# Norms between layers: tokens times the scale vector, turned by products with a diagonal of the tokens' factors

## The chip, the cores and the metric

The kernel runs on one core of a Trainium2 chip. The metric is the time of one execution in device microseconds (us). The engines are TensorE (PE in the profile, with its weight loads as PEld), VectorE (DVE), ScalarE (ACT), GpSimd (POOL) and SyncE (SP, which issues most DMAs). SBUF is the memory on the core, PSUM the one that TensorE writes its products to.

## The reference

One launch computes two transformer blocks on 256 tokens of 1024 features. The first has two layers (a mixture of block attention and compressed attention, then a forgetting attention) with a squared-ReLU MLP each; the second a gated MLP, a hybrid of differential attention and a state-space scan, and another gated MLP. All of it is in 32-bit floats. What matters here is the norm that stands between one layer and the next:

```python
def rmsnorm(x, g):
    xf = x.astype(jnp.float32)
    y = xf * lax.rsqrt(jnp.mean(xf * xf, axis=-1, keepdims=True) + RMS_EPS)
    return (y * g.astype(jnp.float32)).astype(x.dtype)

    for layer in range(DEPTH):
        hn = rmsnorm(h, mix_norm[layer])
        ...
        h = h + moba_nsa_mixer(hn, ...)
        ...
        h = h + sqrelu_mlp(rmsnorm(h, mlp_norm[layer]), mlp_w1[layer], mlp_w2[layer])
```

Each token is divided by the root of its mean square (one factor per token), multiplied by a vector of 1024 gains (one per feature), and goes into the next layer's first product. In the second block the branch is normed too before it is added to h.

## The kernel before

The residual x lies in SBUF with the tokens on the partitions, as two halves t = 0 and t = 1 of 128 tokens. A product on TensorE sums over partitions, so a layer's input has to be turned: features on the partitions, tokens along the row. The turned input `xx` has eight chunks of 128 features, each twice: a rounded part and a rest (`split`, L386 to 388: ACT copies the rounded part, DVE subtracts it for the rest), because all large products run in a reduced 32-bit type (fp32r) as a sum of rounded-by-rounded, rounded-by-rest and rest-by-rounded. Weights stream in by chunks of 1 MB (`raw`, DMA from SP), and are split likewise into `whi` (ACT, L387) and `wlo` (DVE, L388). Each product is issued by `mm` (L214). Fp32r products of 512 columns and of 256 columns make up nearly all of PE's work.

Between two layers:

- `finish` (L967) ends a layer: the last products of t = 0 (`part(0)`), its `epi`, the last products of t = 1, the turn of t = 0, the `epi` of t = 1. It leaves the turn of t = 1 as `late_turn` to the next layer.
- `epi` adds the layer's products to x (L990, or scales by a further norm, L427, in the second block), and calls `prenorm` (L431). It takes the sum of squares of the two 512-feature halves on ACT (`xn<-x`, L410), adds the two and the epsilon on DVE (`ms`, L423), raises that to -1/2 on POOL (`rs<-ms`, L416), and multiplies x by that factor and the gain on DVE, each half in one instruction (`xn<-x,rs,gain`, L427).
- `turn` (L391) turns xn chunk by chunk: PE transposes four chunks of 128x128 into one PSUM bank (L397, `ps_p<-cst,xn` or `ps_b<-cst,xn`, where cst holds the identity), then `split` writes them to xx; twice for eight chunks.
- `begin` (L310 on) starts the next layer: it runs the first three weight groups on t = 0, two of them into the bank pair ps_o and the third into a ps_b bank, then calls `late_turn`, then runs the three on t = 1.

There are six such boundaries (two token halves each, twelve turns). The first norm of the program, the state-space part's own norm and the output's are made elsewhere.

The tile framework's scheduler sets the order of instructions on each engine ahead of the run, from dependencies, its own cost estimates and priorities: `soon(300)` raises the priority of the turns and epis. Each engine then works its list strictly in that order. Buffers come from pools with a fixed count: P tiles (128x384) nine (`PB`), xn two, ps_b four banks, ps_p two.

Of the kernel before, what the change touches and what calls it, by code (L numbers as in the profile page):

```python
# [12 lines left out]
OP = mybir.AluOpType  # L13
# [7 lines left out]
PB = 9  # L21
# [93 lines left out]
class Kern:  # L115
# [274 lines left out]
    def turn(self, src, xx, k0, t, n=4, tag="b", than=None):  # L390


        w = min(n, 4)
        for b in range(0, n, w):
            ps = self.bank(tag)
            for k in range(w):
                i = self.nc.tensor.transpose(ps[:, k * 128:k * 128 + 128],  # L397
                                             src[:, (b + k) * 128:(b + k) * 128 + 128], self.ident)
                if than is not None:
                    self.later(i, than)  # L400
            s = slice(k0 + b, k0 + b + w)
            self.split(xx[:, s, t * 128:t * 128 + 128], xx[:, s, 256 + t * 128:256 + t * 128 + 128],
                       ps[:, :w * 128].rearrange("p (k n) -> p k n", k=w))
# [25 lines left out]
    H = (slice(0, 512), slice(512, 1024))  # L429

    def prenorm(self, t, G, eps):  # L431
        x = self.x[:, t, :]
        xn = self.t([128, 1024], "xn", 2)
        r = self.rstd([x[:, s] for s in self.H], xn, eps)
        for s in self.H:
            self.scaled(xn[:, s], x[:, s], r, G[:, s])
        return xn

    def first_norm(self, t, G, eps):

# [1229 lines left out]
```

## Time and profile before

| | us |
|---|---|
| median of 3 runs | 1206.33 (1205.54 to 1206.60) |
| the profiled execution | 1205.98 |
| its span, first to last instruction | 1203.6 |
| mean granted clock of TensorE | 0.999 of full |

The page gives for each engine the time in which it was busy; a line of the timeline has the start, the time taken by the group, the engine, the line of the kernel, the operation, output and inputs by their names, the shapes and the count of instructions, and in brackets how long the engine had been idle before and what ended that. PE is the engine with the most busy time; the end of a matrix product is modelled, so that two products in a row overlap in the trace. The rows that matter stand two sections below.

### The profile page before, as it was taken

The numbers are of one execution on the slowest core, as the hardware profiler recorded it, in microseconds if no ns is written. First come the engines' busy times: TensorE is split into PE (matmuls) and PEld (weight loads), VectorE is DVE, ScalarE is ACT, GpSimd is POOL, SyncE is SP. The second block draws the span as 40 slices with busy tenths as digits, with TensorE's granted clock in tenths as the row PEclk, the third lists the DMA queues.
The fourth block names the chain that finished last, engine by engine and source line by source line (L and its number), as shares of the span: only waits on it lengthen the run. The fifth ranks groups of instructions, "written<-read, shape, count | busy, mean of one in ns | idle before, by whom it ended". The sixth has DMA issues, their size and how long they took to land.

```text
span 1203.6 us, 17736 instructions
## 1 busy us (share of the span) xinstructions
PE 1176.9 (98%) x6890; PEld 1002.3 (83%) x6890; DVE 795.7 (66%) x1442; ACT 658.5 (55%) x1221; POOL 86.8 (7%) x119
## 2 busy tenths in 40 slices
PE   8999999999999999999999999999999999999997
PEld 6878688888887878888888888887987778888886
DVE  6685666666667657566657665676888876666663
ACT  5675554545455645454546555564764755555552
POOL 2200000000000000000002000003234020000000
PEclk9999999999999999999999999999999999999999
DMA  8645255555456334555544655562543235555550
GB/s 300 227 159 192 106 192 177 194 189 187 165 197 241 106 118 176 183 205 177 197 186 154 237 178 202 180 222 95 199 151 123 88 135 181 187 197 180 199 182 35
DMA packets 32245, 210.71 MB, mean 175 GB/s; under 512 B 3761, under 2 KB 4561, under 8 KB 8226
## 3 DMA queue, kind: packets, MB, share of 16 engines
q1 hardware_dynamic: 29360, 201.06, 47.1%
q0 software_dynamic: 2512, 8.27, 2.1%
q8 instruction: 54, 0.88, 0.3%
q10 hardware_dynamic: 290, 0.27, 0.1%
q14 instruction: 29, 0.24, 0.1%
HBM read 208.22 MB, written 1.09 MB: 174 GB/s over the span
## 4 chain that ended last, share of the span: by engine, by line
PE 85%; DVE 6%; ACT 3%; issue 2%; POOL 1%; DMA 1%; SPq 0%; POOLq 0%; DVEq 0%; ACTq 0%
PE ps_b L214 39%; PE ps_p L214 26%; PE ps_o L214 15%; DVE wlo L388 2%; PE ps_o L218 2%; ACT whi L387 1%; PE ps_b L538 1%; PE ps_p L397 1%; DMA raw<-in_w_e 1%; ACT xn L410 1%; ACT P L561 1%; DVE xn L427 1%; POOL rs L416 1%; DMA T<-c_dram 1%; PE ps_b L397 0%
## 5 line engine op out<-in xcount | busy, mean ns | idle before, releaser
L388 DVE TENSOR_TENSOR wlo<-raw,whi 128x1024 fp32r<-128x1024 f32 (+1 forms) x365 | 443.5, 1233 | 232.8 <-ACT whi L387 232.0
L387 ACT ACTIVATE whi<-raw 128x1024 fp32r<-128x1024 f32 (+1 forms) x367 | 376.7, 1048 | 182.2 <-PE ps_p L214 89.6
L214 PE MATMUL ps_b<-xx,whi 128*128 128x512 f32 x1024 | 361.5, 394 | 0.0
L214 PE MATMUL ps_b<-xx,wlo 128*128 128x256 f32 x1024 | 289.1, 282 | 0.0
L214 PEld LDWEIGHTS ps_b<-xx,whi 128*128 128x128 f32 x1024 | 192.3, 188 | 43.8
L214 PEld LDWEIGHTS ps_b<-xx,wlo 128*128 128x128 f32 x1024 | 192.5, 188 | 1.7
L214 PE MATMUL ps_p<-xx,whi 128*128 128x256 f32 (+2 forms) x800 | 146.1, 286 | 0.6 <-DVE fz L1284 0.5
L214 PEld LDWEIGHTS ps_p<-xx,whi 128*128 128x128 f32 (+2 forms) x800 | 120.9, 185 | 5.9 <-issue 4.1
L214 PE MATMUL ps_p<-xx,wlo 128*128 128x256 f32 x384 | 108.2, 282 | 0.0
L214 PE MATMUL ps_b<-whi,xx 128*128 128x256 f32 (+2 forms) x440 | 102.5, 320 | 1.4 <-ACT xx L387 1.4
L214 PE MATMUL ps_p<-whi,xx 128*128 128x512 f32 x232 | 82.9, 414 | 1.6 <-DVE xx L388 1.0
L416 POOL TENSOR_TENSOR rs<-ms,mhalf 128x1 f32<-128x1 f32 x22 | 14.8, 672 | 903.8 <-DVE ms L423 894.6
L214 PEld LDWEIGHTS ps_b<-whi,xx 128*128 128x128 f32 x440 | 73.2, 188 | 7.7 <-ACT xx L387 1.6
L214 PEld LDWEIGHTS ps_p<-xx,wlo 128*128 128x128 f32 x384 | 72.3, 188 | 0.6 <-issue 0.6
L214 PE MATMUL ps_p<-whi,q 128*128 128x512 f32 x216 | 71.6, 391 | 0.0
L214 PE MATMUL ps_o<-whi,q 128*128 128x512 f32 x216 | 71.5, 392 | 0.0
L214 PE MATMUL ps_b<-wlo,xx 128*128 128x256 f32 (+2 forms) x220 | 70.7, 322 | 0.3 <-DVE wlo L388 0.2
L242 ACT ACTIVATE tB<-ps_b 128x256 f32<-128x256 f32 x128 | 47.7, 373 | 40.5 <-PE ps_b L214 40.5
L214 PE MATMUL ps_p<-whi,k 128*128 128x512 f32 x184 | 61.5, 394 | 0.0
L214 PE MATMUL ps_o<-whi,k 128*128 128x512 f32 x184 | 61.1, 393 | 0.0
L243 DVE TENSOR_TENSOR P<-ps_b,tB 128x256 f32<-128x256 f32 x128 | 53.5, 418 | 5.7 <-ACT tB L242 5.7
L214 PEld LDWEIGHTS ps_p<-whi,xx 128*128 128x128 f32 x232 | 43.3, 188 | 16.5 <-issue 5.5
(322 smaller groups left out, 1678.7 us busy)
## 6 DMA issues: line engine op xcount, KB each, us to landing
raw<-in_w_m SPq DMA_DIRECT2D x64, 1024.0 KB, 4.9
raw<-in_w_s SPq DMA_DIRECT2D x16, 1024.0 KB, 4.9
raw<-in_w_o SPq DMA_DIRECT2D x12, 1024.0 KB, 5.1
raw<-in_w_f1g SPq DMA_DIRECT2D x11, 1024.0 KB, 4.9
raw<-in_w_f1u SPq DMA_DIRECT2D x11, 1024.0 KB, 4.8
raw<-in_w_f1d SPq DMA_DIRECT2D x11, 1024.0 KB, 4.9
raw<-in_w_f2g SPq DMA_DIRECT2D x11, 1024.0 KB, 4.9
raw<-in_w_f2u SPq DMA_DIRECT2D x11, 1024.0 KB, 4.8
```

Of the source, the lines that this page charges most:

```text
L214: self.last_mm = self.nc.tensor.matmul(out, l, r, start=start, stop=stop)
L218: self.nc.tensor.matmul(out, l, r, start=start, stop=False, skip_group_check=True)
L242: nc.scalar.activation(tmp[:m], ps[:m, 256:512], AF.Copy)
L243: nc.vector.tensor_add(dst, ps[:m, :256], tmp[:m])
L387: self.nc.scalar.activation(hi, src, AF.Copy)
L388: self.nc.vector.tensor_sub(lo, src, hi)
L397: i = self.nc.tensor.transpose(ps[:, k * 128:k * 128 + 128], src[:, (b + k) * 128:(b + k) * 128 + 128], self.ident)
L410: self.nc.scalar.activation(junk[:, h * 512:h * 512 + 512], halves[h], AF.Square, scale=1.0 / 32, accum_out=ss[:, h:h + 1])
L416: self.last_pow = self.nc.gpsimd.tensor_tensor(r, m, self.mhalf, op=OP.pow)
L427: self.nc.vector.scalar_tensor_tensor(dst, src, r, G, op0=OP.mult, op1=OP.mult)
L538: nc.tensor.transpose(b[:, c * 128:c * 128 + 128], P[:, c * 128:c * 128 + 128], self.ident)
L561: nc.scalar.activation(P[:, o:o + w], P[:, o:o + w], AF.Exp, scale=-1.0, bias=nm[:, j:j + 1], accum_out=sums[:, x, j:j + 1])
```

## The change

In `prenorm` the multiplication by the gain is taken apart from that by the token's factor. The first half of x times the gain is made ahead of `ms`, the second half between `ms` and the result of the power, and the 128 factors multiply the identity, which gives a diagonal matrix `d`. `turn` takes the pair: instead of transposing a chunk, PE multiplies it, as the stationary operand, with `d`, which gives the turned chunk with every token scaled. This is an unreduced 32-bit product with 128 columns.

```diff
-                i = self.nc.tensor.transpose(ps[:, k * 128:k * 128 + 128],
-                                             src[:, (b + k) * 128:(b + k) * 128 + 128], self.ident)
+                o, i = ps[:, k * 128:k * 128 + 128], src[:, (b + k) * 128:(b + k) * 128 + 128]
+                if d is None:
+                    i = self.nc.tensor.transpose(o, i, self.ident)
+                else:
+                    i = self.nc.tensor.matmul(o, i, d, start=True, stop=True)
...
     def prenorm(self, t, G, eps):
-        x = self.x[:, t, :]
+
+        x, nc = self.x[:, t, :], self.nc
         xn = self.t([128, 1024], "xn", 2)
-        r = self.rstd([x[:, s] for s in self.H], xn, eps)
-        for s in self.H:
-            self.scaled(xn[:, s], x[:, s], r, G[:, s])
-        return xn
+        ss = self.squares([x[:, s] for s in self.H], xn)
+        m = self.t([128, 1], "ms", 4)
+        a, b = self.H
+        nc.vector.tensor_tensor(xn[:, a], x[:, a], G[:, a], op=OP.mult)
+        nc.vector.scalar_tensor_tensor(m, ss[:, 0:1], eps, ss[:, 1:2], op0=OP.add, op1=OP.add)
+        r = self.power(m)
+        nc.vector.tensor_tensor(xn[:, b], x[:, b], G[:, b], op=OP.mult)
+        d = self.t([128, 384], "P", PB)[:, :128]
+        nc.vector.tensor_scalar(d, self.ident, r, None, op0=OP.mult)
+        return xn, d
```

Lines of the changed kernel: the product is L402, the squares L414, the power L420, the two multiplies by the gain L442 and L445, `ms` L443, the diagonal L447; lines behind them are 11 further on.

The scheduler puts out another order. On DVE, at the first boundary, both token halves stand so before (x takes the layer's products from ps_p and ps_b, `ms` and `xn` belong to prenorm, `xx` to the turn, `wlo` to the weights):

```order
L990 TENSOR_TENSOR x<-x,ps_p 128x512 x2
L423 SCALAR_TENSOR_TENSOR ms<-ss 128x1
L427 SCALAR_TENSOR_TENSOR xn<-x,rs,gain 128x512 x2
L388 TENSOR_TENSOR wlo<-raw,whi 128x1024
L388 TENSOR_TENSOR xx<-ps_p,xx 128x4x128
L990 TENSOR_TENSOR x<-x,ps_b 128x512
L388 TENSOR_TENSOR xx<-ps_p,xx 128x4x128
L990 TENSOR_TENSOR x<-x,ps_b 128x512
L388 TENSOR_TENSOR wlo<-raw,whi 128x1024
L423 SCALAR_TENSOR_TENSOR ms<-ss 128x1
L388 TENSOR_TENSOR wlo<-raw,whi 128x1024
L427 SCALAR_TENSOR_TENSOR xn<-x,rs,gain 128x512 x2
```

And so in the changed kernel, at the same boundary on DVE, as far as the diagonal of t = 1:

```order
L442 TENSOR_TENSOR xn<-x,gain 128x512
L443 SCALAR_TENSOR_TENSOR ms<-ss 128x1
L445 TENSOR_TENSOR xn<-x,gain 128x512
L447 TENSOR_SCALAR P<-cst,rs 128x128
L388 TENSOR_TENSOR wlo<-raw,whi 128x1024
L388 TENSOR_TENSOR xx<-ps_p,xx 128x4x128
L388 TENSOR_TENSOR wlo<-raw,whi 128x1024
L1001 TENSOR_TENSOR x<-x,ps_b 128x512 x2
L388 TENSOR_TENSOR xx<-ps_p,xx 128x4x128
L388 TENSOR_TENSOR wlo<-raw,whi 128x1024
L442 TENSOR_TENSOR xn<-x,gain 128x512
L443 SCALAR_TENSOR_TENSOR ms<-ss 128x1
```

One multiply by the gain now precedes `ms`, one follows it directly, and the diagonal stands where the two scalings stood. For t = 1 three splits of weights instead of two, and a multiply, stand between the first norm and the second's `ms`.

On PE, at the fourth boundary (from the first block's last MLP to the second block's first), the turn of t = 1 stood before among the first products of t = 1, behind 24 into ps_o, 16 into ps_b, 24 into the other ps_o bank and 4 more:

```order
L214 MATMUL ps_o<-wlo,xx 128x256
L214 MATMUL ps_o<-whi,xx 128x256
L214 MATMUL ps_b<-wlo,xx 128x256
L214 MATMUL ps_b<-whi,xx 128x256 x2
L214 MATMUL ps_b<-wlo,xx 128x256
L397 MATMUL ps_p<-cst,xn 128x128 x4
L214 MATMUL ps_b<-whi,xx 128x256
L397 MATMUL ps_p<-cst,xn 128x128 x4
L214 MATMUL ps_b<-whi,xx 128x256
```

In the changed kernel it stands on PE, at the same boundary, so:

```order
L214 MATMUL ps_b<-wlo,xx 128x256
L214 MATMUL ps_b<-whi,xx 128x256
L402 MATMUL ps_p<-P,xn 128x128 x8
L214 MATMUL ps_o<-whi,xx 128x256
L214 MATMUL ps_o<-wlo,xx 128x256
L214 MATMUL ps_o<-whi,xx 128x256 x2
```

The turn now stands whole, between the 24 products into ps_b and the 24 into ps_o, 20 products earlier. At the first and third boundary it moved likewise to behind 24 products into ps_o and 12 into ps_b, at the second eight products (512 columns) and at the sixth two products earlier. The t = 0 turns stay where they were, or one product earlier (first, fourth, fifth boundary).

## Rows read from the trace of the kernel before

**Rows 1.** The page: busy time and share of the span of each engine; the clock granted to TensorE in tenths, in forty slices; the share of each engine in the chain of work that ended last.

```profile
PE 1176.9 (98%) x6890; PEld 1002.3 (83%) x6890; DVE 795.7 (66%) x1442; ACT 658.5 (55%) x1221; POOL 86.8 (7%) x119
...
PEclk9999999999999999999999999999999999999999
...
PE 85%; DVE 6%; ACT 3%; issue 2%; POOL 1%; DMA 1%; SPq 0%; POOLq 0%; DVEq 0%; ACTq 0%
```

**Rows 2.** Groups of PE's instructions by line and tile: count, busy us in all, mean ns of one, idle before. The first is a transposition, the second a plain 32-bit product of the same shape.

```profile
L1344 PE MATMUL ps_b<-cst,k 128*128 128x128 f32 x16 | 2.4, 272 | 0.0
...
L214 PE MATMUL ps_b<-k 128*128 128x128 f32 x8 | 1.3, 289 | 0.0
```

**Rows 3.** The timeline of the state-space part, where both stand one behind the other: six weight loads for plain products in a row, then four transpositions.

```profile
886.97 0.74 PEld L214 LDWEIGHTS ps_b<-k 128*128 128x128 f32 x6
...
887.98 0.60 PE L1344 MATMUL ps_b<-cst,k 128*128 128x128 f32 x4
```

**Rows 4.** The timeline at the first boundary, t = 0: products of 512 columns, the sum of squares, the power, the two scalings, the turn (start, us, engine, and idle time before with what ended it).

```profile
146.21 0.62 PE L214 MATMUL ps_b<-whi,xx 128*128 128x512 f32 x2
...
146.67 0.39 PE L214 MATMUL ps_b<-wlo,xx 128*128 128x512 f32 x1
...
146.75 0.16 DVE L423 SCALAR_TENSOR_TENSOR ms<-ss 128x1 f32<-128x1 f32 x1 [0.81 <-ACT xn L410]
...
147.00 0.57 POOL L416 TENSOR_TENSOR rs<-ms,mhalf 128x1 f32<-128x1 f32 x1 [32.10 <-DVE ms L423]
...
147.60 1.41 DVE L427 SCALAR_TENSOR_TENSOR xn<-x,rs,gain 128x512 f32<-128x512 f32 x2 [0.69 <-POOL rs L416]
...
148.41 1.32 PE L397 MATMUL ps_p<-cst,xn 128*128 128x128 f32 x8 [0.18 <-DVE xn L427]
149.07 0.42 PEld L397 LDWEIGHTS ps_p<-cst,xn 128*128 128x128 f32 x4 [0.24 <-DVE xn L427]
```

**Rows 5.** Groups of DVE's instructions: a 128x128 tile times one value per token, and the sum of 512 elements a row from SBUF with as many from PSUM.

```profile
L579 DVE TENSOR_SCALAR P<-P,prec 128x128 f32<-128x128 f32 x40 | 12.3, 307 | 0.6
...
L990 DVE TENSOR_TENSOR x<-x,ps_p 128x512 f32<-128x512 f32 x8 | 5.2, 682 | 1.2 <-PE ps_p L214 1.2
```

**Rows 6.** The power on POOL: its least, median and longest ns, and the timeline at t = 1 of the first and of the third boundary, where a split of weights on DVE (two inputs from SBUF) runs as it starts.

```profile
L416 POOL TENSOR_TENSOR rs<-ms,mhalf x22: 542/558/1459, 5.2 to 1198.2; 128x1 f32<-128x1 f32 x22
...
154.07 0.16 DVE L423 SCALAR_TENSOR_TENSOR ms<-ss 128x1 f32<-128x1 f32 x1
...
154.15 1.22 DVE L388 TENSOR_TENSOR wlo<-raw,whi 128x1024 fp32r<-128x1024 f32 x1
...
154.32 1.46 POOL L416 TENSOR_TENSOR rs<-ms,mhalf 128x1 f32<-128x1 f32 x1 [6.75 <-DVE ms L423]
...
459.66 1.22 DVE L388 TENSOR_TENSOR wlo<-raw,whi 128x1024 fp32r<-128x1024 f32 x1
...
459.89 1.39 POOL L416 TENSOR_TENSOR rs<-ms,mhalf 128x1 f32<-128x1 f32 x1 [6.84 <-DVE ms L423]
```

**Rows 7.** The timeline: the turns of t = 0 at the other five boundaries, in order.

```profile
329.22 0.63 PE L397 MATMUL ps_b<-cst,xn 128*128 128x128 f32 x4 [0.45 <-DVE xn L427]
...
453.89 0.66 PE L397 MATMUL ps_p<-cst,xn 128*128 128x128 f32 x4 [0.43 <-DVE xn L427]
...
635.30 1.29 PE L397 MATMUL ps_b<-cst,xn 128*128 128x128 f32 x8 [0.97 <-DVE xn L427]
...
823.84 1.29 PE L397 MATMUL ps_b<-cst,xn 128*128 128x128 f32 x8 [0.41 <-DVE xn L427]
...
1007.13 0.66 PE L397 MATMUL ps_p<-cst,xn 128*128 128x128 f32 x4 [0.60 <-DVE xn L427]
```

**Rows 8.** The timeline at the fourth boundary, t = 1: the start of the second 24 products into ps_o, the chain of the norm, and the turn.

```profile
646.75 0.34 PE L214 MATMUL ps_o<-whi,xx 128*128 128x256 f32 x1
...
648.35 0.16 DVE L423 SCALAR_TENSOR_TENSOR ms<-ss 128x1 f32<-128x1 f32 x1 [0.79 <-ACT xn L410]
...
648.66 0.56 POOL L416 TENSOR_TENSOR rs<-ms,mhalf 128x1 f32<-128x1 f32 x1 [0.23 <-DVE ms L423]
...
649.25 1.42 DVE L427 SCALAR_TENSOR_TENSOR xn<-x,rs,gain 128x512 f32<-128x512 f32 x2 [0.74 <-POOL rs L416]
...
650.18 0.60 PE L397 MATMUL ps_p<-cst,xn 128*128 128x128 f32 x4
```

**Rows 9.** The timeline: PE's instructions beside the turns of t = 1 at the other boundaries (first, second, third, fifth twice, sixth), and the longest wait for DVE in mid-program.

```profile
155.59 0.39 PE L214 MATMUL ps_o<-whi,xx 128*128 128x256 f32 x1 [0.36 <-ACT P L1071]
...
340.61 0.60 PE L397 MATMUL ps_p<-cst,xn 128*128 128x128 f32 x4
...
461.14 0.39 PE L214 MATMUL ps_o<-whi,xx 128*128 128x256 f32 x1 [0.36 <-ACT P L1071]
...
836.21 0.39 PE L214 MATMUL ps_o<-whi,xx 128*128 128x256 f32 x1 [0.69 <-ACT v L1446]
...
837.29 0.66 PE L397 MATMUL ps_p<-cst,xn 128*128 128x128 f32 x4 [0.34 <-DVE xn L427]
...
899.19 0.55 PE L214 MATMUL ps_o<-gain,P 128*128 128x64 f32 x3 [2.16 <-DVE P L1396]
...
1016.64 0.63 PE L397 MATMUL ps_p<-cst,xn 128*128 128x128 f32 x4 [0.44 <-DVE xn L427]
```

More of the change, by code (lines that the diff above doesn't have):

```diff
@@ L393, in turn @@
         w = min(n, 4)
+        src, d = src if isinstance(src, tuple) else (src, None)
         for b in range(0, n, w):
```

## Prediction

> **What bounds the kernel now.** I read the page's busy shares first, then its chain, then the groups of instructions by tile, then the timeline around each place that the diff touches. TensorE (PE) is busy 98% of the span, 85% of the chain that ended last is PE, and the clock row shows 9 in all forty slices [rows 1], so the chip granted its full level, 2.4 GHz, throughout. DVE has a third of the span free and ACT almost half. So two things count: what PE issues more or less, and how long it stands before a turn. The profiled execution took 1205.98 us, 0.35 below the median of 1206.33; the sum is made against 1205.98.
>
> **PE's own work.** At six boundaries between layers, two token halves of eight chunks each are turned: 6 x 2 x 8 = 96 transpositions become 96 plain 32-bit products, whose moving operand is the diagonal. A transposition is one record per instruction; four of them take 0.60 us, one 0.272, so they start (0.60 - 0.272)/3 = 0.109 us apart [rows 2, 3]. The kernel already has plain 32-bit products of the same shape: the chunks from `k` into ps_b, of which the program issues four, and the trace shows eight records [rows 2], two per product. The weight loads of six such records, 0.188 us each, take 0.74 us, so records start (0.74 - 0.188)/5 = 0.110 us apart [rows 3]. A product is thus 2 x 0.11 = 0.22 us against 0.11, and 96 x 0.111 = **+10.7 us**. It is on the path: nothing on PE covers PE. Bounds: if a new product cost one record, 0; if each were four, 96 x 0.327 = +31.4. The middle is the nearest row: same type, shape and place.
>
> The Trainium skill (TensorE: Matmul & The Clock Gate, section Terms) calls the transposing mode four times faster for FP32. By that the term would be +31.4 us and the sum 1240.5. The trace disagrees: two records at a transposition's pace, a factor of two.
>
> **The chain before a turn, t = 0.** At the first boundary [rows 4]: ms on DVE at 146.75 for 0.16, the power on POOL at 147.00 for 0.57, the scaling of both halves on DVE at 147.60 for 1.41 (0.71 a half), first transposition at 148.41. After the change the two multiplies by the gain no longer need the power, and behind it stands only the diagonal. The page has a 128x128 multiply by one value per token on DVE at 0.307 us [rows 5]. On paper the turn starts 0.71 - 0.31 = 0.4 us earlier, at 148.0.
>
> But the order puts the second multiply (x and gain, both in SBUF) straight behind ms, ahead of the power on POOL. Where the trace has such a DVE instruction at work as the power starts, the power takes 1.46 and 1.39 us instead of 0.56: it ended at 155.78 and 461.28, each 0.40 to 0.41 us behind the end of that DVE instruction (155.37, 460.88) [rows 6]. The multiply takes about 0.7 us by the 512-element rows [rows 5]. So it runs from 146.9 to 147.6, the power ends at 148.0, the diagonal at 148.3, and PE starts at about 148.4, where it starts now. I take 0.1 us earlier; bounds: 0.4 earlier (the power undisturbed) and 0.3 later (the multiply 0.2 longer than I take it, the diagonal 0.2 longer). The Trainium skill (SBUF — State Buffer, Who interferes with whom) has the same rule: a VectorE instruction with two SBUF inputs and a GpSimd instruction that reads SBUF exclude each other, and whichever starts second waits in full. By this rule, and by the rows, a gain of 0.4 at each wait is lost.
>
> The six t = 0 turns now wait a shown 0.18 to 0.97 us [rows 4, 7]; each costs 0.16 more than shown, since a pair of 512-column products is drawn 0.62 long while what follows it starts 0.46 later (146.21 to 146.67 [rows 4]: 0.23 a product). Six starts 0.1 earlier: -0.6. All eight chunks now need one diagonal, so the second group's wait (0.24 shown at the first boundary, about 0.2 at two others) goes: -0.6. At three boundaries the order puts the turn one 512-column product earlier, which then stands behind it: +0.7. Sum **-0.5**.
>
> **The chain before a turn, t = 1.** These turns were placed by the scheduler inside the first products of the next stage, often where nothing waits. The new order moves them. The clearest is the fourth boundary: before, the turn stood behind 24 products into ps_o, 16 into ps_b, 24 into ps_o and 4 more; now behind 24 into ps_o and 24 into ps_b, 20 products or 2.4 us earlier at 0.12 each (28 of them from 646.75 to 650.18 [rows 8]). It gets there at 646.75 + 8 x 0.12 = 647.7. Its chain isn't earlier: ms at 648.35, the multiply to 649.2, the power to 649.6, the diagonal to 649.95, PE at 650.05 [rows 8]. So PE waits 2.3 us where it waited for nothing, and what is queued behind the turn on PE is the whole next stage.
> The others, as new wait minus old. First boundary: the order on DVE puts a split (1.22) and the first multiply (0.7) more ahead of ms, and the turn behind 36 products; I estimate 0.7, and the wait for the copy of ps_o that the old order had in front (0.36 shown, 0.52 with the 0.16) and 0.19 at the turn go: 0.0. Third: the same figures with no wait at the turn: +0.2. Second: the turn stands eight 512-column products earlier (1.8 us) against a chain that was ready as PE came (340.61): +0.6. Fifth: 0.34 and 0.69 shown before, with 0.16 each 1.35 in all, and I estimate as much again: 0. Sixth: two products earlier and a split ahead on DVE, 0.6 before (0.44 shown) and 1.1 now: +0.5 [rows 9]. Sum 0.0 + 0.2 + 0.6 + 2.3 + 0 + 0.5 = **+3.6**. These five are estimates on a chain read once; the bounds are -3.5 (all waits at t = 1 gone) and +8 (every turn as late as the fourth's 2.3, less what is there).
>
> **DVE, ACT, POOL, DMA.** Two scalings of 0.71 [rows 4] become two multiplies of 0.68 and a diagonal of 0.31 [rows 5]: some +0.25 us on DVE at each of 12 places, 3 in all, under a PE that is the bound; at no cost but in the chains above. The squares are the same. The diagonal takes one of nine P buffers; none of the rows waits for one to come free, and were one late, PE would wait with the diagonal, which the upper bound of t = 1 covers. The weight queue keeps its order.
>
> **The sum.** 10.7 - 0.5 + 3.6 = +13.8 us: 1205.98 + 13.8 = **1219.8 us**, slower by 1.1%. The longest new wait, 2.3 us, is hardly longer than one that the trace has (2.16 us, with the clock row at 9 around it [rows 1, 9]), so I expect no lower clock.
>
> **Rivals.**
> 1. The power is not held up. The multiply may end before the power's operands are read, or the power go first. Then each of 12 waits is up to 0.4 shorter, -4 to -5: 1215. For it: only two pairs among the rows show the hold-up, both with a longer DVE instruction. Against: there that instruction started as close behind ms (154.07 and 154.15) as the multiply will, and ahead of the power (154.32) [rows 6].
> 2. A product costs four transpositions: 10.7 becomes 31.4, and the time 1240. For it: the shape was read at one place of the program alone. Against it: the eight records at 0.11 [rows 2, 3].
> 3. The early turns cost more: at t = 1 the wait delays the next stage's first evacuations, PE meets the next bank unreleased, and each of the twelve loses 0.3 to 0.5 more: +4 to +6, 1225. For it: PE already waits for such an evacuation, 0.36 shown at two boundaries [rows 9].
> 4. The other side, faster: the diagonal product costs one record, as the old transposition does (its moving operand is also an array of 128 columns), and the power is undisturbed, so PE's work is unchanged and each t = 0 wait falls by 0.4: 12 x -0.4 = -4.8 and +3.6 of placing less 0.5 to 2 gives 1203 to 1204. It decides if a product takes under 0.13 us (then 96 x 0.02 = 1.9 is less than the waits give back). The eight records speak against it.
> 5. The change does not shorten what it is about, and the product cost hides in waits that PE has anyway: no wait stands beside most products (the turns follow each other back to back, 0.11 apart), so this would need the t = 1 waits to be absorbed: within 2.4 us of before.
>
> **How the numbers follow.** Forecast 0.58, rival 1 0.22, rival 3 0.09, rival 2 0.05, rival 4 0.03, rival 5 0.03. The forecast's own range is 1216 to 1223, from the bounds of the t = 1 estimates that I hold likely (half of +3.6 to twice). With rivals 1 and 3 it reaches from 1212 to 1226, and leaves out rivals 2, 4 and 5 and some tails, 0.2 at most. About 0.2% (2.4 us) is what a measurement of this kernel can tell from no change. Faster 0.03, within 0.2% 0.04, slower 0.93.
>
> **What would show it.** Product groups with two records each (192 in all), about 1.77 us per turn of eight where it was 0.87; power instructions of about 1.0 us at the boundaries, ending 0.4 behind the multiply; PE waiting 2 to 2.5 us for the diagonal at the fourth boundary's second half, and under 1 us at most others; no new lines among PE's releasers but the diagonal. Wrong would be: one record or four per product, powers of 0.56 us, t = 1 turns that wait for nothing, or a clock row below 9.

## The result, and the profile after

| | before | changed |
|---|---|---|
| median of the runs (us) | 1205.93 (4 runs, 1205.47 to 1206.60) | 1220.40 (4 runs, 1219.82 to 1224.30) |
| ratio | | 1.012, 95% interval 1.0102 to 1.0137 |
| profiled execution, its span | 1205.98, 1203.6 | 1224.30, 1222.5 |
| mean granted clock of that execution | 0.999 | 0.992 |

The change makes the kernel 14.5 us slower; 1219.8 was forecast. The profiled execution is the longest of the four, at the lowest clock; the other three took 1219.8 to 1220.7 at 0.996. A second set of four executions of the changed kernel (the seventh experiment) gave 1220.35.

The page of the changed kernel, its lines for busy time, granted clock and chain, as in [rows 1]:

```profile
PE 1194.2 (98%) x6986; PEld 1020.9 (84%) x6986; DVE 797.5 (65%) x1454; ACT 658.3 (54%) x1221; POOL 87.5 (7%) x119
...
PEclk8999999999999999999999999999999999999999
...
PE 84%; DVE 6%; issue 3%; ACT 3%; POOL 2%; DMA 1%; SPq 0%; POOLq 0%; DVEq 0%; ACTq 0%
```

PE has 96 records more (6986 against 6890) and 17.3 us more busy time: the kernel is bound where it was. The first slice of the clock now shows an 8, which the prediction named as a sign of being wrong. It comes from a stretch at the lower level from 15 to 22 us, where both kernels still run the same instructions in the same order (the first turn by products starts at 152 us); the page of the seventh experiment, the same kernel, has 9 in all slices. A single fall of a few microseconds elsewhere is not seen in tenths of a slice of 30 us.

The groups of the products that took the place of the transpositions, and on DVE the second multiply and the diagonal (count, busy us, mean ns, idle before with what ended it):

```profile
L402 PE MATMUL ps_p<-P,xn 128*128 128x128 f32 x144 | 19.7, 294 | 6.1 <-DVE P L447 6.1
...
L402 PE MATMUL ps_b<-P,xn 128*128 128x128 f32 x48 | 6.1, 280 | 1.9 <-DVE P L447 1.9
```

```profile
L445 DVE TENSOR_TENSOR xn<-x,gain 128x512 f32<-128x512 f32 x12 | 8.2, 684 | 0.0
...
L447 DVE TENSOR_SCALAR P<-cst,rs 128x128 f32<-128x128 f32 x12 | 3.6, 298 | 5.4 <-POOL rs L420 5.4
```

144 + 48 = 192 records for 96 products: two each. PE's idle time before them is 8.0 us, all of it for the diagonal, and DVE in turn waits 5.4 us for the power.

The power, by its least, median and longest ns:

```profile
L420 POOL TENSOR_TENSOR rs<-ms,mhalf x22: 547/858/947, 5.1 to 1217.1; 128x1 f32<-128x1 f32 x22
```

Its median went from 558 ns [rows 6] to 858, since the twelve at the boundaries all take 0.86 to 0.95 us. Nine of them took 0.54 to 0.57 before, and three at t = 1, where a split ran beside them, 1.39 to 1.46. The timeline at the first boundary, t = 0, answers to [rows 4]:

```profile
150.61 0.16 DVE L443 SCALAR_TENSOR_TENSOR ms<-ss 128x1 f32<-128x1 f32 x1
150.69 0.69 DVE L445 TENSOR_TENSOR xn<-x,gain 128x512 f32<-128x512 f32 x1
150.86 0.95 POOL L420 TENSOR_TENSOR rs<-ms,mhalf 128x1 f32<-128x1 f32 x1 [32.09 <-DVE ms L443]
...
151.84 0.29 DVE L447 TENSOR_SCALAR P<-cst,rs 128x128 f32<-128x128 f32 x1 [0.47 <-POOL rs L420]
...
152.18 1.05 PE L402 MATMUL ps_p<-P,xn 128*128 128x128 f32 x7 [0.32 <-DVE P L447]
```

The multiply starts on the heels of ms and ends at 151.38; the power, started meanwhile, ends 0.43 behind it. From the start of ms to the first product it is 1.57 us, where it was 148.41 - 146.75 = 1.66: the shorter chain gave 0.09. At the other five boundaries the time from the start of the power to the turn of t = 0 is 0.08 to 0.15 us shorter.

The timeline at the fourth boundary, t = 1, answers to [rows 8]:

```profile
656.66 0.63 ACT L414 ACTIVATE xn<-x 128x512 f32<-128x512 f32 x1 [1.97 <-DVE x L431]
...
657.32 0.63 ACT L414 ACTIVATE xn<-x 128x512 f32<-128x512 f32 x1
...
658.06 1.28 ACT L1089 ACT_TABLE_LOAD   x1
...
658.39 0.87 POOL L420 TENSOR_TENSOR rs<-ms,mhalf 128x1 f32<-128x1 f32 x1 [0.23 <-DVE ms L443]
659.29 0.29 DVE L447 TENSOR_SCALAR P<-cst,rs 128x128 f32<-128x128 f32 x1 [0.46 <-POOL rs L420]
659.36 0.38 ACT L1089 ACTIVATE P<-ps_o 128x256 f32<-128x256 f32 x1
659.63 2.72 PE L402 MATMUL ps_p<-P,xn 128*128 128x128 f32 x13 [2.04 <-DVE P L447]
```

PE waits 2.04 us for the diagonal. Two things are to be seen beside it. ACT is idle for 1.97 us before the squares and then loads its table and evacuates ps_o (copies it out of PSUM) behind them; before, it did that first:

```profile
644.98 1.28 ACT L1078 ACT_TABLE_LOAD   x1
...
646.93 0.63 ACT L410 ACTIVATE xn<-x 128x512 f32<-128x512 f32 x1 [0.28 <-DVE x L427]
```

And the turn takes long: 13 records of it in 2.72 us. The stretches from 658 us on, with the granted clock third from the end of each line, and then a stretch of before, behind its turn:

```profile
658.00:660.00 2.00, 0.36 (x3) 0.37 (x4) 1.12 (x4) 1.71 (x3) 1.77 (x4) 1.00 1.01 418
660.00:662.00 2.00, 2.00 (x13) 2.00 (x12) 0.04 (x1) 0.60 (x1) 2.00 (x5) 0.53 0.85 342
662.00:664.00 2.00, 2.00 (x13) 2.00 (x13) 0.98 (x2) 0.87 (x2) 1.01 (x2) 0.61 0.92 247
664.00:666.00 2.00, 2.00 (x20) 2.00 (x19) 0.35 (x1) 0.00 (x0) 0.00 (x0) 1.00 0.35 54
```

```profile
650.00:652.00 2.00, 2.00 (x19) 1.98 (x19) 1.56 (x4) 1.18 (x3) 2.00 (x5) 1.00 0.83 307
```

Right behind the wait TensorE ran for between three and four microseconds at the lower of its two levels, 1.2 GHz, and lost (1 - 0.53) x 2 + (1 - 0.61) x 2 = 1.7 us of full-speed work. In before all stretches from 646 to 656 us stand at 1.00.

### The profile page after: what moved, and what is told of

It reads as the page before. It is cut to its first block, busy times and chain, and to the rows that moved or that the text cites. A ratio compares the mean times of both kernels' runs of the same rounds, so it can differ in the third digit from the quotient of the medians.

```text
span 1222.5 us, 17931 instructions
## 1 busy us (share of the span) xinstructions
PE 1194.2 (98%) x6986; PEld 1020.9 (84%) x6986; DVE 797.5 (65%) x1454; ACT 658.3 (54%) x1221; POOL 87.5 (7%) x119
## 4 chain that ended last, share of the span: by engine, by line
PE 84%; DVE 6%; issue 3%; ACT 3%; POOL 2%; DMA 1%; SPq 0%; POOLq 0%; DVEq 0%; ACTq 0%
PE ps_b L214 38%; PE ps_p L214 25%; PE ps_o L214 14%; DVE wlo L388 2%; PE ps_o L218 2%; PE ps_p L402 1%; ACT whi L387 1%; POOL rs L420 1%; PE ps_b L549 1%; ACT xn L414 1%; DMA raw<-in_w_e 1%; ACT P L572 1%; DMA T<-c_dram 1%; DVE xn L442 0%; POOL P L1377 0%
## 5 line engine op out<-in xcount | busy, mean ns | idle before, releaser
L420 POOL TENSOR_TENSOR rs<-ms,mhalf 128x1 f32<-128x1 f32 x22 | 16.3, 739 | 921.7 <-DVE ms L427 553.4
```

The lines of the kernel that those rows point to most:

```text
L420: self.last_pow = self.nc.gpsimd.tensor_tensor(r, m, self.mhalf, op=OP.pow)
```

## The experiments

**1. The new chain with transpositions.** The power is raised to the exponent 0, so that the diagonal is the identity and PE can use it in the transposing mode; the tokens' factors are left out of the output. Two turns are tied to a product, to keep them about where the change has them.

```diff
-                    i = self.nc.tensor.matmul(o, i, d, start=True, stop=True)
+                    i = self.nc.tensor.transpose(o, i, d)
...
-        r = self.power(m)
+        r = self.power(m, self.zero)
```

> The new chain of the norm (gain first, then the power, then the diagonal) is kept, but PE turns by transpositions: the power is to the exponent 0, so the diagonal is the identity, and the tokens' factors are left out of the output. PE waits for the diagonal as before; the t = 1 turns stand where the change puts them, or some 37 products behind the first at the first and third boundary. If the 96 products cost a second record each, their 10.7 us go: 1220.2 - 10.7 = 1209.5 us (1208 to 1211), a turn of eight takes 0.87 to 1.1 us, and 96 records stand there. If the time went into waits and the order of the work, the products being nearly free, it stays at 1216 or more.

1208.34 us (10 runs, 1206.18 to 1212.03); ratio to before 1.0011 (0.9996 to 1.0027). With the same chain and the same wait of 2.2 us at the fourth boundary, taking away the second records takes 12 us away (1220.40 - 1208.34).

```profile
L409 PE MATMUL ps_p<-P,xn 128*128 128x128 f32 x72 | 9.7, 278 | 5.3 <-DVE P L454 5.3
...
L409 PE MATMUL ps_b<-P,xn 128*128 128x128 f32 x24 | 3.2, 276 | 1.9 <-DVE P L454 1.9
```

96 records, and still 7.2 us of waiting for the diagonal. What is left to the new chain and the new order is 1.7 us by the medians, with an interval that includes none.

**2. Products with the identity, old chain.** The other half of the same division.

```diff
-        return xn
+        return xn, self.ident
...
-                    i = self.nc.tensor.transpose(o, i, self.ident)
+                    i = self.nc.tensor.matmul(o, i, d, start=True, stop=True)
```

> The old norm (the scaling by gain and factor ahead of the turn), but the turn is a plain 32-bit product with the identity instead of a transposition. If the product's second record is the main cost: 1205.9 + 10.7 = 1216.6 us (1215.5 to 1218), 192 records, turns of eight at 1.77 us. If the cost is in the new chain and placing: 1206 to 1209.

1216.52 us (4 runs, 1215.83 to 1217.80), 1.008 of before (1.0065 to 1.0095): +9.9 us. Its first turn in the timeline:

```profile
147.49 2.05 PE L402 MATMUL ps_p<-cst,xn 128*128 128x128 f32 x16 [0.18 <-DVE xn L431]
```

16 records a turn. From start to start the twelve turns of this run take 21.3 us, those of before 10.2: +11.1 by the trace, against +9.9 by the times, whose interval reaches from 7.8 to 11.5. (The order changed a little too: at t = 1 of the first and third boundary PE waits 0.47 shown for xn, where it waited 0.36 for ACT P.)

**3. The second multiply behind the diagonal.** The multiply of the second half is tied on DVE behind the diagonal, and the turns of t = 1 at the first and third boundary behind a product.

```diff
-        nc.vector.tensor_tensor(xn[:, b], x[:, b], G[:, b], op=OP.mult)
...
-        nc.vector.tensor_scalar(d, self.ident, r, None, op0=OP.mult)
+        i = nc.vector.tensor_scalar(d, self.ident, r, None, op0=OP.mult)
+        self.later(nc.vector.tensor_tensor(xn[:, b], x[:, b], G[:, b], op=OP.mult), i)
```

> The changed kernel with the second multiply by the gain behind the diagonal on DVE, so that nothing with two SBUF inputs starts ahead of the power at the six t = 0 norms and at two of t = 1; at the other four of t = 1 the order puts a split of weights (1.22 us, two SBUF inputs) there. If the hold-up is by the DVE instruction at work as the power starts: eight powers of 0.55 to 0.57 us and four of 1.4 to 1.5; PE's waits at t = 0 shrink by 0.3 to 0.4 each, those of the four grow by 0.5: 1219 us (1217.5 to 1220.5). If the new power is slower for another reason (the operands' place, the start of POOL): 0.86 to 0.95 us in all twelve and the waits unchanged or longer.

1220.34 us (4 runs, 1219.55 to 1224.52): as the changed kernel, and not the 1 us less. The mechanism came out as forecast, though. The first boundary, t = 0 and t = 1:

```profile
151.80 0.57 POOL L427 TENSOR_TENSOR rs<-ms,mhalf 128x1 f32<-128x1 f32 x1 [32.09 <-DVE ms L450]
152.40 0.28 DVE L453 TENSOR_SCALAR P<-cst,rs 128x128 f32<-128x128 f32 x1 [0.69 <-POOL rs L427]
...
160.56 1.22 DVE L395 TENSOR_TENSOR wlo<-raw,whi 128x1024 fp32r<-128x1024 f32 x1
160.73 1.46 POOL L427 TENSOR_TENSOR rs<-ms,mhalf 128x1 f32<-128x1 f32 x1 [8.36 <-DVE ms L450]
```

Eight powers take 0.54 to 0.57 us with DVE idle at their start, four take 1.39 to 1.46 beside a split. So the hold-up goes with the DVE instruction at work as the power starts. From ms to the first product it is now 152.74 - 151.56 = 1.18 us. But the scheduler, which sees the shorter chain, moved the t = 0 turns one or two 512-column products (0.23 us each) forward, and the waits there stayed: 0.34 to 1.36 us from start to start, as against 0.45 to 1.21. And at t = 1 of the first and third boundary, where the tied turns no longer wait, PE waits for a split of weights instead, 1.03 and 0.81 us shown, longer than the 0.28 for the diagonal in the changed kernel:

```profile
161.83 0.39 PE L216 MATMUL ps_b<-wlo,xx 128*128 128x256 f32 x1 [1.03 <-DVE wlo L395]
```

So this run doesn't price the hold-up: what it gave at t = 0 went into the order, and its other waits grew.

**4. The turns of t = 1 held back.** Each is tied on PE behind a named product of t = 0.

```diff
+HOLDS = [None] + [(1, 5), (0, 18), (1, 5), (1, 18), (1, 12), (1, 8)]
...
-                self.late_turn()
+                h = HOLDS[len(self.begun)]
+                self.begun.append(t)
+                self.late_turn(mms[h[0]][h[1]] if h else None)
```

> The changed kernel with the t = 1 turns held back on PE, each behind as many more products of t = 0 as its wait lasted (0.45, 0.43, 0.45, 2.20, 1.51 and 0.99 us of excess at the six boundaries, 6.0 in all). If these waits are a loss of their own, most of it comes back: 1215 us (1214 to 1216.5). If the next stage then waits for the turned input instead (the splits behind the turn are 1.3 us later against the first product of t = 1), it stays: 1218.5 to 1220.5, with PE waiting for ACT or DVE xx behind the turns.

1217.90 us (4 runs, 1216.40 to 1218.99): 2.4 us come back, not 5. The turns of t = 1 no longer wait at any of the six boundaries; at the fifth and sixth older waits for ACT came back in their place (0.85 and 0.46 from start to start). At the fourth:

```profile
653.76 1.28 ACT L1096 ACT_TABLE_LOAD   x1
655.06 0.38 ACT L1096 ACTIVATE P<-ps_o 128x256 f32<-128x256 f32 x1
...
655.49 0.39 PE L216 MATMUL ps_o<-whi,xx 128*128 128x256 f32 x1 [2.21 <-ACT P L1096]
```

PE waits as long at the next products, for ps_o to be evacuated, and at 662.59 another 0.54 us for the split of the turned input (DVE xx). The diagonal's lateness alone isn't what stops PE there: two waits end at almost the same time (in the changed kernel the diagonal at 659.58, the evacuation at 659.74), and each covers the other.

**5. The evacuation ahead of the squares.** Run 4, and at the fourth boundary ACT's squares of t = 1 are tied behind the evacuation; the norm of t = 1 is issued after the first products of t = 0 for that.

```diff
-        ss = self.squares([x[:, s] for s in self.H], xn)
+        ss = self.squares([x[:, s] for s in self.H], xn, self.evac)
...
-            nc.scalar.activation(sg[t], ps, AF.Silu)
+            i = nc.scalar.activation(sg[t], ps, AF.Silu)
+            if t == 0 and len(self.begun) == 4:
+                self.evac = i
```

> As the run with the turns held back, and at the fourth boundary ACT again evacuates ps_o (table load and P) ahead of the squares of t = 1, as in the kernel before; the turn there stands behind all 72 products of t = 0. If PE's 2.3 us at that boundary come from ACT's order (the evacuation behind the squares), the wait of 2.37 us for ACT P goes, and at most 1 us for the turned input takes its place: 1217.9 - 1.4 = 1216.5 us (1215.5 to 1217.5). If the diagonal's lateness is the cause by itself, PE still waits 1.5 us or more there and the time stays at 1217.5 to 1218.5.

1217.62 us (4 runs, 1213.61 to 1220.97). The wait for ACT is gone, and a third one stands there:

```profile
655.88 0.39 PE L217 MATMUL ps_b<-wlo,xx 128*128 128x256 f32 x1 [2.35 <-DVE wlo L396]
```

Its cause is in the same trace:

```profile
650.75 0.22 DVE L1298 TENSOR_TENSOR lamp<-par 128x64 f32<-128x64 f32 x1 [4.14 <-DMA par<-in_lam]
```

With the norm issued elsewhere, the scheduler put this small instruction, which waits for a DMA, ahead of the splits of weights on DVE, and all of them came later. So the run made a wait of its own, and doesn't answer its question; what the place costs is answered by the eighth and ninth.

**6. The gain first, with transpositions.** The kernel before, with the first half multiplied by the gain ahead of ms, and by the factor behind the power; an attempt to keep the shorter chain without the products.

```diff
-        r = self.rstd([x[:, s] for s in self.H], xn, eps)
-        for s in self.H:
-            self.scaled(xn[:, s], x[:, s], r, G[:, s])
+        self.nc.vector.tensor_tensor(xn[:, a], x[:, a], G[:, a], op=OP.mult)
+        self.nc.vector.scalar_tensor_tensor(m, ss[:, 0:1], eps, ss[:, 1:2], op0=OP.add, op1=OP.add)
+        r = self.power(m)
+        i = self.nc.vector.tensor_scalar(xn[:, a], xn[:, a], r, None, op0=OP.mult)
+        self.scaled(xn[:, b], x[:, b], r, G[:, b])
```

> The kernel before, with its transpositions, but the first half of x times the gain is made ahead of the sum of squares, and behind the power stands only a multiply of that half by the token's factor (one input from SBUF, 128x512); the second half is scaled as before. If that multiply takes 0.36 to 0.5 us instead of 0.71, the second half is ready 0.2 to 0.35 earlier and eight waiting turns give back 1.5 to 2.5 us: 1204.5 against 1206.3 (at the edge of what can be told). If the order moves the turns forward by as much, as it did when the second multiply was put last, the time stays within 1 us.

1207.19 us (12 runs, 1205.48 to 1212.41), 1.0011 of before (0.9997 to 1.0025): no gain. The second of the two expectations held; the chain at the first boundary:

```profile
146.03 0.57 POOL L416 TENSOR_TENSOR rs<-ms,mhalf 128x1 f32<-128x1 f32 x1 [32.10 <-DVE ms L438]
146.62 0.49 DVE L440 TENSOR_SCALAR xn<-xn,rs 128x512 f32<-128x512 f32 x1 [0.69 <-POOL rs L416]
...
147.17 0.66 PE L397 MATMUL ps_p<-cst,xn 128*128 128x128 f32 x4 [0.38 <-DVE xn L440]
```

The factor takes 0.49 us instead of 0.71, and PE waits longer than it did (0.38 shown, 0.18 in [rows 4]), since the turn was moved forward.

**7. The changed kernel once more.** No edit.

> The changed kernel itself, once more, for the granted clock: if the lower clock of its first four executions (0.992 to 0.996) belongs to it, all stand at 0.993 to 0.997 again, against 0.997 to 0.999 of before, and a wait above 2 us is followed by a stretch at the lower level; if that was the chip's state, both kernels spread over the same clocks and at one clock the difference is 10.7 + 1.6 = 12.3 us.

1220.35 us (4 runs, 1220.03 to 1224.73), clocks of 0.996 three times and 0.992 once, just as the first four. The wait at the fourth boundary (now at 655.48) has the same stretch behind it:

```profile
654.00:656.00 2.00, 0.52 (x4) 0.52 (x5) 0.97 (x3) 1.58 (x2) 1.77 (x4) 1.00 1.03 412
656.00:658.00 2.00, 2.00 (x13) 2.00 (x13) 0.56 (x1) 0.60 (x1) 2.00 (x5) 0.59 0.91 277
658.00:660.00 2.00, 2.00 (x12) 2.00 (x11) 0.83 (x2) 0.87 (x2) 0.86 (x2) 0.55 0.79 281
```

That is one of two such stretches in this profile; the other, at 912 us, stands behind the wait of 2.17 us in the state-space part that before has too [rows 9]. The kernel before, in the 64 executions that were run beside the experiments, had a mean clock at or under 0.996 in 18; the changed kernel in all 8. At one clock, 0.996, the changed kernel's executions took 1219.8 to 1220.7 and those of before 1207.7 to 1208.6: 12.1 us apart, close to the 12.3 expected. So the lower clock is commoner in the changed kernel, but before has it too, and neither of the two expectations holds alone.

**8. and 9. One turn undone, and one turn alone.** The old form at t = 1 of the fourth boundary only, in the changed kernel; and the new form there only, in the kernel before.

```diff
+def OLD(t, done):
+    return t == 1 and done == 3
...
     def prenorm(self, t, G, eps):
+        if OLD(t, self.done):
+            xn = self.t([128, 1024], "xn", 2)
+            r = self.rstd([self.x[:, t, s] for s in self.H], xn, eps)
+            for s in self.H:
+                self.scaled(xn[:, s], self.x[:, t, s], r, G[:, s])
+            return xn
```

(Run 9 has `not (t == 1 and done == 3)`.)

> The changed kernel with one turn of the twelve put back to the old form (scaling by gain and factor, transpositions): that of t = 1 at the fourth boundary; the order there falls back to the one before (evacuation of ps_o ahead of the squares, the turn behind 63 products of t = 0). Eight second records less are 0.9 us. If the order at this place costs its wait of 2.2 us by itself, 1220.3 - 0.9 - 2.2 = 1217.2; if the wait also brings the stretch at the lower clock behind it (about 1.7 us), 1215.5 (1214.5 to 1216.5) and mean clocks of 0.997 and above in most executions. If the wait only stood in place of a later one, 1219.4.

1216.33 us (6 runs, 1214.88 to 1219.86): 4.0 us come back from one turn of twelve, with a mean clock of 0.997 or 0.998 in all six. The order of before is back (the turn behind 68 products, not 63), and no wait at the turn:

```profile
652.38 1.28 ACT L1101 ACT_TABLE_LOAD   x1
653.68 0.39 ACT L1101 ACTIVATE P<-ps_o 128x256 f32<-128x256 f32 x1
654.33 0.63 ACT L419 ACTIVATE xn<-x 128x512 f32<-128x512 f32 x1 [0.27 <-DVE x L436]
...
657.54 0.60 PE L405 MATMUL ps_p<-cst,xn 128*128 128x128 f32 x4
```

The traces give the parts. From the turn of t = 0 at the fourth boundary to that at the fifth it is 193.96 us in the changed kernel (193.93 in run 7) and 189.32 here: 4.6 us, of which 0.9 are the second records of one turn and 2.2 the wait; the remaining 1.5 are the stretch at the lower clock.

> The kernel before with the change at that one turn only (t = 1, fourth boundary), where the order then is that of the changed kernel. Eight second records are 0.9 us. With the wait of 2.2 us by itself 1206.3 + 3.1 = 1209.4; with a stretch at the lower clock behind it in most executions 1211 (1210 to 1212) and mean clocks at or under 0.996. If the wait only stands in place of a later one, 1207.2.

1209.69 us (12 runs, 1207.48 to 1212.42), 1.0016 of before (1.0003 to 1.0028): +3.0 us by the medians, +0.4 to +3.4 by the interval of the ratio. That fits the 0.9 + 2.2 without the clock, but by the times alone the 0.9 is not excluded. The trace decides. Its profiled execution has both the wait and the fall behind it:

```profile
649.48 1.79 PE L407 MATMUL ps_p<-P,xn 128*128 128x128 f32 x12 [2.05 <-DVE P L458]
```

```profile
650.00:652.00 2.00, 2.00 (x15) 2.00 (x14) 0.69 (x1) 0.60 (x1) 2.00 (x5) 0.69 0.93 272
652.00:654.00 2.00, 2.00 (x11) 2.00 (x11) 0.69 (x1) 0.87 (x2) 0.86 (x2) 0.50 0.80 288
```

From the turn of t = 0 at the fourth boundary to that at the fifth it is 193.07 us, where before has 823.84 - 635.30 = 188.54 [rows 7]: 4.5 = 0.9 + 2.2 + 1.4 for the fall. Nothing of it is won back later: behind the fifth boundary the two traces differ by the fall in the state-space part alone (33.89 against 31.14 us from its long wait to the next), and by 0.1 us behind the sixth.

Of its twelve executions only four have a mean clock at or under 0.996, and of the 17 of before beside them five: the wait didn't make a low mean clock commoner. So the wait is a loss of its own in either setting. Whether the clock falls behind it is another matter: it did in four profiles with this wait (the changed kernel twice, runs 1 and 9) and behind the 2.35 us of run 5, not in run 4, where the same length was waited for ACT, and not in run 3, where it was 1.90 us from start to start. What decides it stays open.

**10. The kernel before with its turns held back.** What the holds of run 4 do for the transpositions, with those of t = 0 too: LEFT says how many of the last products of t = 1 are left behind the turn.

```diff
+LEFT = [9, 17, 9, 16, 18, 5]
+HOLDS = [None] + [None, None, None, None, (1, 8), (1, 3)]
...
-                self.turn(a, xx, 0, 0, 8, tag)
+                self.turn(a, xx, 0, 0, 8, tag, log[-r - 1] if r else None)
```

> The kernel before (scaling ahead, transpositions) with eight of its twelve turns held back on PE behind two to six products that stood behind them, so that the scaled tokens are there as PE arrives: all six of t = 0 (waits of 0.34 + 0.17, 0.61, 0.59, 1.14 + 0.2, 0.57 + 0.2 and 0.77 us from start to start, 4.6 in all) and those of t = 1 at the fifth and sixth boundary (0.8 and 0.6). If these waits are a loss by themselves: 1206.4 - 5 = 1201.5 us (1200.5 to 1203), below both kernels. If PE then waits for the turned input of the next stage instead, 1204 to 1206.5, with new waits on ACT or DVE xx behind the turns.

1204.16 us (12 runs, 1203.55 to 1209.52), 0.9981 of before (0.9967 to 0.9995): 2.7 us faster by the medians (0.6 to 4.0 by the interval), the fastest of the kernels here, and about half of the gain that was expected. At t = 0 the waits are gone:

```profile
147.37 1.20 PE L406 MATMUL ps_p<-cst,xn 128*128 128x128 f32 x8
...
151.85 0.39 PE L217 MATMUL ps_b<-whi,xx 128*128 128x256 f32 x1 [0.96 <-ACT whi L396]
```

The second line is where a part of the rest went, some 1.2 us: at the first and third boundary ACT's split of weights now stands behind the splits of the turned input, and PE waits 1.1 us from start to start for it (0.5 before, for another evacuation).

## Why the prediction was right

- *The second records.* Forecast +10.7 us, from the plain products of the state-space part [rows 2, 3]. The trace shows the two records; putting transpositions in their place takes away 12 us (run 1), putting products into the kernel before adds 9.9 (run 2). In each of the two runs the order changed a little as well, and both give the same size. Rival 2 (four transpositions each, +31.4) and rival 4 (one record) fall.
- *The power held up.* Forecast about 1.0 us for it and a turn 0.1 us earlier; measured 0.86 to 0.95, and 0.09 at the first boundary. Run 3 shows the cause by taking it away at eight places and lengthening it at four. By the Trainium skill (SBUF — State Buffer, Who interferes with whom) a VectorE instruction with two SBUF inputs contends with a GpSimd instruction that reads SBUF, and the later of the two waits for the whole of the earlier. The trace agrees: the power ended 0.43 us behind the multiply, and 0.40 to 0.41 behind the splits [rows 6]. Rival 1 did not come: all twelve powers were held up. That its 4 to 5 us could be had without the hold-up is not shown: run 3, with eight of twelve powers undisturbed, didn't gain, as the turns of t = 0 moved forward and other waits grew.
- *The waits at t = 0.* Forecast -0.5 us: 3.98 us in the changed kernel from start to start, against some 4.6 before: -0.6.
- *The waits at t = 1.* Forecast +3.6. New waits of 0.45, 0.43, 0.45, 2.20, 1.51 and 0.99 us were forecast as 0.7, 0.6, 0.7, 2.3, 1.35 and 1.1: 6.0 where the estimates make 6.75. Less what stood there before this is about +2.7. The step was a little too large, in the single estimates and not in the fourth boundary that it rested on. The range was not worked out as it says: half of +3.6 to twice gives 1218.0 to 1223.4, where 1216 to 1223 is stated. The 3 us forecast for DVE came to 1.8 of busy time.
- *The fourth boundary.* The wait of 2.3 us came (2.04 shown, 2.20 from start to start), and runs 8 and 9 show that it costs that much. The reason given was half of it: the earlier place of the turn. The other half is ACT's order, which run 4 brought out: the evacuation behind the squares would have stopped PE for as long.
- *The clock.* This step failed. "So I expect no lower clock" rested on one wait of 2.16 us without a fall [rows 9]. That one was an exception: nine of the twelve profiles here, runs 2, 6 and 10 without any diagonal among them, have a fall behind this wait, and 51 of the 64 executions of the kernel before have a mean clock under the 0.999 of its profile. In the changed kernel's profiles the wait at the fourth boundary has a fall behind it too, which costs 1.5 us (run 8), and the one in the state-space part costs 1.2 (last section); together 2.7, where the forecast has nothing. By the measured terms: 11.1 for the products by the trace of run 2 (9.9 by its time), -0.6 and +2.7 for the waits, and 2.7 for the two falls make 15.9 (14.7) of the 14.5; the terms come from different executions and don't add up closer than that. That the time came within 0.6 us of the forecast owes something to luck, two misses of opposite sign: about 1 us too much for the waits, nothing for the clock.

Rival 5 (hidden cost) fell with run 2. Rival 3 (a cascade) did not appear in the changed kernel: nothing but the diagonal is new among PE's longer waits. Run 4 shows how near it was: at the fourth boundary PE would have waited as long for ps_o.

## What to carry to other kernels

Before moving a multiplication into a matrix product, look in the trace for the same type and shape: a plain 32-bit product was two records where a transposition was one, and these 10 to 11 us are more than all the waits at turns that a shorter chain could have taken away here (some 4.6 us at t = 0 and 3 at t = 1). A chain that ends at a wait can be cheaper to wait out elsewhere: moving the consumer a few products back (run 10) gave 2.7 us, while three ways of shortening the chain (the change, runs 3 and 6) gave none: each time the scheduler also moved the consumer forward. And where one wait is removed, ask what else ends at that time: at the fourth boundary there were two, and the attempt to remove both made a third.

## What the runs showed of the hardware

- Mean clock and time go together across executions of one kernel: before took 1204.4 to 1205.7 us at 0.999 and 1211.0 to 1212.2 at 0.993, about 1.1 us for each 0.001. Two of 64 stand outside of this, 1210.1 and 1210.8 us at 0.998. Differences of a few us between two kernels are best read at one clock.
- A wait of PE of about 2.2 us is, in some executions and not in others, followed by a few microseconds at or near the lower level (0.50 to 0.69 in stretches of 2 us). Behind the wait of 2.16 us in the state-space part [rows 9] nine profiles of twelve have such a fall within 2 us; before and run 5 have none there, and run 8 has one 43 us later.
- What a fall costs can be read from a stretch that is the same in all kernels. From that wait to PE's next one, for DVE k, it is 31.14 or 31.15 us in the three profiles without a fall in between (before, runs 5 and 8) and 32.31 to 32.43 in eight with one; in run 9, where it lasted twice as long, it is 33.89. That is 1.2 us for one, less than the 1.7 of work lost at the fourth boundary. The lines are of before, and of the changed kernel in run 7:

```profile
930.33 0.41 PE L214 MATMUL ps_o<-gain,P 128*128 128x64 f32 x2 [1.18 <-DVE k L1385]
```

```profile
910.90 0.55 PE L214 MATMUL ps_o<-gain,P 128*128 128x64 f32 x3 [2.17 <-DVE P L1407]
...
943.31 0.41 PE L214 MATMUL ps_o<-gain,P 128*128 128x64 f32 x2 [1.17 <-DVE k L1396]
```

- A multiply of 128x512 by one value per token took 0.498 us on DVE (run 6), where the multiply by factor and gain together took 0.746 in the same run.
